# Column sums over 64 folded rows in one product, and a split reload of stored pages, in a two-layer decoder trunk

## The chip, the cores and the metric

One core of one Trainium2 chip runs the whole program. The metric is the device time of one execution in microseconds (us), the median of several executions; less is better. The kernel before has a median of 1169.38 us over 3 runs (1169.09 to 1169.43).

## What is computed

The input x is 1024 tokens by 1024 features in float32. Layer A is gated linear attention (4 heads, key width 128, value width 256, in chunks), layer B is dilated windowed attention over a shared K/V. Both end in an output product, a residual and a layer norm. What the change touches are sums over features:

```python
# layer A, per head: RMS norm of the head's 256 output features, then gain and gate, then the output product
o = o * lax.rsqrt(jnp.mean(o * o, axis=-1, keepdims=True) + RMS_EPS)
return (o.astype(x.dtype) * jax.nn.silu(g)) @ w_out

# end of both layers
x = layer_norm(DEEPNORM_ALPHA * x + y, ln_g[layer], ln_b[layer])

def layer_norm(x, g, b):
    mu = jnp.mean(x32, axis=-1, keepdims=True)
    xc = x32 - mu
    var = jnp.mean(xc * xc, axis=-1, keepdims=True)
    return xc * lax.rsqrt(var + LN_EPS) * g + b
```

## The kernel before

**Numbers.** Every large product is made from float32r halves: a value is split into a high part (`split_hi`, a copy on ACT that rounds, line 590) and a low part (`split_lo`, a subtraction on DVE or POOL, line 593), and a product is three TensorE instructions, high by high, high by low and low by high (`mm3`, line 620, and the like). Features lie on the partitions, tokens on the free axis, so a sum over features is a sum over partitions. It is made by a product with a 128x128 tile of ones, `onesr`: the tile of partial sums is split, and two products of 128x512, one for the high and one for the low part, add up in one PSUM bank (tag "ms", two buffers). The result stands in all 128 partitions.

**Where sums over partitions are made.** There are 14 of them. `chunks` (line 952) has one for each of the 4 heads and 2 chunks g of 512 tokens: the squares of the head's two output tiles are added, split and summed (lines 978 to 989); `rsqrt_rows` and a multiplication follow, and `finish` (line 995) applies gain and gate. For heads 0 to 2 the result goes to DRAM (`ogA`), for head 3 it is split at once into the pages ogh6/ogl6 and ogh7/ogl7 (the names ogh, ogl in the trace). `out_ln` (line 1035) has two for a half of 512 tokens, one for the mean (name lnA) and one for the variance, through its own `column_sums` (line 1038). It runs for both halves of layer A's end and for the first half of layer B's; the second half of layer B goes by rows (`out_ln_rows`), without such sums.

**The order of the work.** The code records operations; `Sched.order` (line 249) then places them one by one on PE, ACT, DVE, POOL and SP by its own table of costs: of all operations that are ready, the one that can start first goes next, and of several that can start at the same time the one with the lowest number in recording order. `later(n)` shifts that number. An operation recorded on `S.vp` goes to DVE or to POOL, whichever starts it earlier. So any change in one place moves instructions everywhere behind it. Projections of the next head (wA, xs) fill TensorE while a head's own chain runs on the other engines.

**The reload.** The six pages that heads 0 to 2 left in DRAM are loaded, split (ogf to ogh and ogl, kt 0 to 5) and used by layer A's output product. `reload_og` (line 1480) is called in the sequence of head 3 (letter `e`, line 1014), ahead of that head's chunks, and records both halves of 512 tokens at once with `later(-EVAC)`:

```python
for f in ('qg', 'qVg', 'qg', 'vge')[h]:
    {"g": lambda: proj_g(h), "q": lambda: proj_qk(h + 1), "V": proj_v12, "v": lambda: proj_v(3), "e": after}[f]()
for g in range(2):
    chunks(h, g)
    finish(h, g)
```

Behind it, `out_ln` of layer A runs `proj_cols` for each of 8 output tiles over kt 0 to 7 (24 products), first half first; with two "acc" banks TensorE can go through kt 0 to 5 of two tiles before it needs kt 6, which comes from head 3's first chunk. After the second half's 192 products layer B begins with `proj_v0(range(4))`, which needs the normed first half (x1h, x1l, eight pages).

Of the kernel before, what the change touches and what calls it, by code (L numbers as in the profile page):

```python
# [7 lines left out]
F32 = mybir.dt.float32  # L8
FR = mybir.dt.float32r
# [3 lines left out]
AF = mybir.ActivationFunctionType  # L13
# [5 lines left out]
GH = 4  # L19
# [556 lines left out]
def trunk(tc, xT, wP, wA, wA12, wAv3, w2, b2, ng, wO, wK, wV0, wV12, wB, wOB, lng, lnb,  # L576
# [13 lines left out]
    def split_hi(dst, src):  # L590
        S.scalar.activation(dst, src, AF.Copy)

    def split_lo(dst, src, hi):
        S.vp.tensor_sub(dst, src, hi.bitcast(F32))
# [84 lines left out]
    def load_consts():  # L679
# [3 lines left out]
        S.sync.dma_start(lngc, lng)  # L683
        S.sync.dma_start(lnbc, lnb)

    def rsqrt_rows(dst, src_ps, scale, tmp):

        S.scalar.activation(tmp, src_ps, AF.Ln, scale=scale, bias=epsc)
        S.scalar.activation(dst, tmp, AF.Exp, scale=-0.5)
# [13 lines left out]
    def layer_a(t2, t1, after):  # L703
# [116 lines left out]
        def proj_qk(h):  # L820
            new_qk(h)
            project(wA[h, 0], xs, lambda half, acc: evac_q(h, half, acc))
            project(wA[h, 1], xs, lambda half, acc: evac_k(h, half, acc))
# [22 lines left out]
        def proj_v(h):  # L846
            new_v(h)
            project_tok(wAv3, xs, [(j, lambda x, j=j: blk(x, j)) for j in range(NCH)],
                        lambda j, acc: evac_v(h, j, acc))

        def proj_g(h, cc=(0, 1)):
            if 0 in cc:
                new_sg(h)
            for c in cc:
                project(wA[h, 2 + c], xs, lambda half, acc, c=c: evac_g(h, c, half, acc))
            silu(h)
# [95 lines left out]
        def chunks(h, g):  # L952
# [27 lines left out]
                S.scalar.activation(sq[e], po[e], AF.Square)  # L980
                S.vector.tensor_copy(oT[:, e, :], po[e])
            S.vp.tensor_add(sq[0], sq[0], sq[1])
            sh, sl = (t2.tile([128, 512], FR, name="sq", bufs=3) for _ in range(2))
            split_hi(sh, sq[0])
            split_lo(sl, sq[0], sh)
            ss = ps.tile([128, 512], F32, name="ms", bufs=2)
            with S.group():
                S.tensor.matmul(ss, onesr, sh, start=True, stop=False)
                S.tensor.matmul(ss, onesr, sl, start=False, stop=True)
            R = t2.tile([128, 512], F32, name="sq", bufs=3)  # L990
            rsqrt_rows(R, ss, 1.0 / 256.0, sq[0])
            for e in range(2):
# [17 lines left out]
        for h in range(GH):  # L1010
            gate(h)
            levels(h)
            state_prep(h)
            for f in ('qg', 'qVg', 'qg', 'vge')[h]:
                {"g": lambda: proj_g(h), "q": lambda: proj_qk(h + 1), "V": proj_v12, "v": lambda: proj_v(3), "e": after}[f]()
            for g in range(2):
                chunks(h, g)
                finish(h, g)


    def small(name, tag, bufs, dt=F32, shape=(128, 512)):
# [13 lines left out]
    def out_ln(layer, r, w_of, res, emit):  # L1035
        n = r.stop - r.start

        def column_sums(x):
            hi, lo = (small("sum", "d", 4, FR)[:, :n] for _ in range(2))
            split_hi(hi, x)  # L1040
            split_lo(lo, x, hi)
            acc = ps.tile([128, 512], F32, name="ms", bufs=2)[:, :n]
            with S.group():
                S.tensor.matmul(acc, onesr, hi, start=True, stop=False)
                S.tensor.matmul(acc, onesr, lo, start=False, stop=True)
            return acc

        rt = []
# [1 line left out]
        for et in range(NK):  # L1050
# [9 lines left out]
                S.vp.tensor_add(lnA, rt[0], rt[1])  # L1060
            elif et > 1:
                S.vp.tensor_add(lnA, lnA, t)
        sm = column_sums(lnA)
        mean = small("mean", "d", 4)[:, :n]
        S.scalar.activation(mean, sm, AF.Copy, scale=1.0 / D)
        a2 = None
        for et in range(NK):
# [4 lines left out]
                a2 = s2  # L1072
            else:
                S.vp.tensor_add(a2, a2, s2)
        sv = column_sums(a2)
        R = small("R", "d", 4)[:, :n]
        t0 = small("t0", "t2", 2)[:, :n]
        rsqrt_rows(R, sv, 1.0 / D, t0)
# [398 lines left out]
        return U  # L1477


    def reload_og():  # L1480
        with S.later(-EVAC):
            for half in range(2):
                for kt in range(6):
                    load_og(ogA[kt], kt, p0, lambda: small("ogf", "a", 13), (half,))

    layer_a(t2, t1, reload_og)
    x1s = []
# [133 lines left out]
```

## Time and profile before

| | |
|---|---|
| median of 3 runs | 1169.38 us |
| the profiled execution | 1169.77 us |
| its span, first to last instruction | 1167.9 us |
| mean granted TensorE clock | 0.998 |
| PE busy | 1156.2 us, 99% |
| DVE, ACT, POOL busy | 768.3, 483.6, 162.6 us |
| chain that ended last | PE 97%, DVE 2%, DMA 1% |

The profiled execution takes 1.87 us more than its span, which lies around the program's own instructions. Matmuls are pipelined: one of 512 columns is shown with some 390 ns, and the next starts 0.227 us behind it. So what an instruction costs TensorE is read from start to start, never from the duration shown. All operations are recorded by one helper, so they share line 441, and groups are told apart by the names of their tiles.

### The profile page before, as it was taken

How to read it: one execution, taken by the hardware profiler on the slowest of the kernel's cores; microseconds unless marked ns; L12 is line 12 of the kernel's file. 1: busy time of each engine (PE TensorE's matmuls, PEld its weight loads, DVE VectorE, ACT ScalarE, POOL GpSimd, SP SyncE). 2: the span in 40 equal slices, each digit the busy share in tenths (PEclk: the TensorE clock that was granted, in tenths of full speed). 3: DMA queues.
4: the chain of work that ended last, by engine and by line, in shares of the span. 5: the costliest groups of instructions: out<-in, count | busy, mean ns of one | idle time of the engine just before them, and what ended most of it. 6: DMA issues, size and time to landing. Idle time of an engine off the chain costs nothing.

```text
span 1167.9 us, 19404 instructions
## 1 busy us (share of the span) xinstructions
PE 1156.2 (99%) x7684; PEld 981.4 (84%) x7684; DVE 768.3 (66%) x1494; ACT 483.6 (41%) x1021; POOL 162.6 (14%) x100
## 2 busy tenths in 40 slices
PE   9999999999999999999999999999999999999997
PEld 8878888889988888888888888888888888888885
DVE  6294953585867597765365657584757676647578
ACT  5364531555464345411214443435333533545242
POOL 1001000202112121221020202020212111103000
PEclk9999999999999999999999999999999999999999
DMA  7211122111143463643611111111141011134544
GB/s 251 71 38 37 56 90 76 52 56 54 57 168 112 142 208 134 198 138 106 207 47 38 46 38 55 38 50 44 38 163 38 20 38 26 32 93 145 180 145 180
DMA packets 93226, 108.17 MB, mean 93 GB/s; under 512 B 44016, under 2 KB 62064, under 8 KB 93136
## 3 DMA queue, kind: packets, MB, share of 16 engines
q1 hardware_dynamic: 93136, 106.94, 29.3%
q8 instruction: 60, 0.98, 0.4%
q14 instruction: 30, 0.25, 0.1%
HBM read 85.74 MB, written 21.17 MB: 92 GB/s over the span
## 4 chain that ended last, share of the span: by engine, by line
PE 97%; DVE 2%; DMA 1%; ACT 0%; issue 0%; SPq 0%; DVEq 0%; ACTq 0%
PE acc L441 64%; PE po L441 10%; PE lv L441 9%; PE vac L441 7%; PE ms L441 5%; PE pro L441 2%; DVE oT L441 1%; DMA xf<-in_xT 1%; DVE X L441 0%; DVE rt L441 0%; ACT sq L441 0%; SPq L441 0%; DVE b L441 0%; DVE diag L441 0%; ACT xh L441 0%
## 5 line engine op out<-in xcount | busy, mean ns | idle before, releaser
L441 PE MATMUL acc<-x1h,wh 128*128 128x512 f32 x608 | 250.5, 412 | 0.0
L441 PE MATMUL acc<-x1h,wl 128*128 128x512 f32 x608 | 237.5, 391 | 0.0
L441 PE MATMUL acc<-x1l,wh 128*128 128x512 f32 x608 | 237.0, 390 | 0.0
L441 ACT ACTIVATE wh<-wf 128x1024 fp32r<-128x1024 f32 (+2 forms) x105 | 108.5, 1034 | 294.8 <-PE acc L441 165.3
L441 POOL TENSOR_TENSOR wl<-wf,wh 128x1024 fp32r<-128x1024 f32 x39 | 93.4, 2395 | 624.0 <-ACT wh L441 488.8
L441 PEld LDWEIGHTS acc<-x1h,wl 128*128 128x128 f32 x608 | 114.1, 188 | 24.5
L441 PEld LDWEIGHTS acc<-x1l,wh 128*128 128x128 f32 x608 | 114.5, 188 | 21.3
L441 PEld LDWEIGHTS acc<-x1h,wh 128*128 128x128 f32 x608 | 114.4, 188 | 21.2
L441 DVE TENSOR_TENSOR wl<-wf,wh 128x1024 fp32r<-128x1024 f32 (+2 forms) x66 | 82.5, 1250 | 66.8 <-ACT wh L441 56.5
L441 ACT ACTIVATE P<-P,sts 128x128 f32<-128x128 f32 (+2 forms) x192 | 81.3, 425 | 63.3 <-DVE sts L441 62.9
L441 PE MATMUL acc<-xh,wh 128*128 128x512 f32 x256 | 102.5, 400 | 0.0
L441 PE MATMUL acc<-xh,wl 128*128 128x512 f32 x256 | 99.9, 390 | 0.0
L441 PE MATMUL acc<-xl,wh 128*128 128x512 f32 x256 | 99.8, 390 | 0.0
L441 DVE TENSOR_TENSOR t<-acc,cosT 128x512 f32<-128x512 f32 x60 | 41.4, 691 | 77.6 <-PE acc L441 77.4
L441 DVE TENSOR_TENSOR t<-acc,sinT 64x512 f32<-64x512 f32 x120 | 82.6, 688 | 1.6
L441 DVE CUSTOM_DVE_ANT_0 P<-lv,bmask 128x256 f32<-128x256 f32 (+1 forms) x128 | 46.8, 380 | 39.1 <-PE lv L441 38.5
L441 DVE TENSOR_TENSOR Q<-t,t 128x512 f32<-128x512 f32 x47 | 69.1, 1471 | 1.5
L441 PE MATMUL lv<-K,Q 128*64 128x64 f32 (+2 forms) x512 | 69.0, 286 | 0.0
L441 PEld LDWEIGHTS lv<-K,Q 128*128 128x128 f32 (+1 forms) x512 | 53.8, 163 | 9.7 <-issue 1.6
L441 PE MATMUL acc<-ogh,wh 128*128 128x512 f32 x152 | 60.2, 396 | 0.0
L441 PE MATMUL acc<-ogl,wh 128*128 128x512 f32 x152 | 59.4, 391 | 0.3 <-DVE ogl L441 0.2
L441 PE MATMUL acc<-ogh,wl 128*128 128x512 f32 x152 | 59.2, 390 | 0.0
(244 smaller groups left out, 2168.7 us busy)
## 6 DMA issues: line engine op xcount, KB each, us to landing
wf<-in_wB SPq DMA_DIRECT2D x32, 512.0 KB
wf<-in_wA SPq DMA_DIRECT2D x24, 512.0 KB
wf<-in_wO SPq DMA_DIRECT2D x16, 512.0 KB
wf<-in_wOB SPq DMA_DIRECT2D x16, 512.0 KB
wf<-in_wV SPq DMA_DIRECT2D x12, 512.0 KB
res<-in_xT SPq DMA_DIRECT2D x16, 256.0 KB
x1d<-rt SPq DMA_DIRECT2D x16, 256.0 KB
out<-rt SPq DMA_DIRECT2D x16, 256.0 KB
```

Of the source, the lines that this page charges most:

```text
L441: getattr(handle[o.eng], meth)(*[conv(a) for a in args], **{k: conv(v) for k, v in kw.items()})
```

## The change

`column_sums` becomes one function for both places, with a second form, `fold`. Folded, ACT copies partitions 64 to 127 of the partial sums down to 0 to 63 of a new tile, `S.vp` adds them in place, ACT makes the high part in partitions 0 to 63 of a tile `parts`, and `S.vp` writes the low part into its partitions 64 to 127. One product with the ones sums both. Ten of the 14 sums take this form: heads 0 to 2 in both chunks (6) and `out_ln` wherever the half starts at token 0 (4). Head 3 and the second half of layer A's end keep two products.

`reload_og` takes the half as an argument. The first half is recorded where both were; the second is recorded behind head 3's first chunk and its `finish`, without the shift.

```diff
+    def column_sums(acc, x, tile, fold):
+        if not fold:
+            hi, lo = tile(FR), tile(FR)
+            split_hi(hi, x)
+            split_lo(lo, x, hi)
+            with S.group():
+                S.tensor.matmul(acc, onesr, hi, start=True, stop=False)
+                S.tensor.matmul(acc, onesr, lo, start=False, stop=True)
+            return
+        t, parts = tile(F32), tile(FR)
+        S.scalar.activation(t[0:64], x[64:128], AF.Copy)
+        S.vp.tensor_add(x[0:64], x[0:64], t[0:64])
+        split_hi(parts[0:64], x[0:64])
+        S.vp.tensor_sub(parts[64:128], x[0:64], parts[0:64].bitcast(F32))
+        S.tensor.matmul(acc, onesr, parts, start=True, stop=True)
...
@@ chunks @@
-            sh, sl = (t2.tile([128, 512], FR, name="sq", bufs=3) for _ in range(2))
-            split_hi(sh, sq[0])
-            split_lo(sl, sq[0], sh)
             ss = ps.tile([128, 512], F32, name="ms", bufs=2)
-            with S.group():
-                S.tensor.matmul(ss, onesr, sh, start=True, stop=False)
-                S.tensor.matmul(ss, onesr, sl, start=False, stop=True)
+            column_sums(ss, sq[0], lambda dt: t2.tile([128, 512], dt, name="sq", bufs=3), h < GH - 1)
...
@@ layer_a, the loop over heads @@
-                {"g": lambda: proj_g(h), "q": lambda: proj_qk(h + 1), "V": proj_v12, "v": lambda: proj_v(3), "e": after}[f]()
+                {"g": lambda: proj_g(h), "q": lambda: proj_qk(h + 1), "V": proj_v12, "v": lambda: proj_v(3), "e": lambda: after(0)}[f]()
             for g in range(2):
                 chunks(h, g)
                 finish(h, g)
+                if h == GH - 1 and g == 0:
+                    after(1)
...
@@ out_ln @@
+            column_sums(acc, x, lambda dt: small("sum", "d", 4, dt)[:, :n], r.start == 0)
...
-    def reload_og():
-        with S.later(-EVAC):
-            for half in range(2):
-                for kt in range(6):
-                    load_og(ogA[kt], kt, p0, lambda: small("ogf", "a", 13), (half,))
+    def reload_og(half):
+        with S.later(0 if half else -EVAC):
+            for kt in range(6):
+                load_og(ogA[kt], kt, p0, lambda: small("ogf", "a", 13), (half,))
```

What the order makes of it is shown at three places.

**DVE, between head 2's second chunk and head 3's first level.** X on 128x8x64 is the operand of the first level's products (first from b, then times q and k); sq is the sum of squares, oT the chunk's output. Before:

```order
L441 TENSOR_TENSOR sq_2958<-sq_2909,sq_2950 128x512
L441 TENSOR_TENSOR X_2968<-b_2866 128x8x64 x2
L441 TENSOR_TENSOR X_2981<-b_2866 128x16x32
L441 COPY v_2885<-acc_2941 128x256
L441 TENSOR_TENSOR oT_2926<-oT_2926,sq_2987 128x512 x2
L441 SCALAR_TENSOR_TENSOR oT_2926<-oT_2926,ngc_120,sg_2553 128x512 x2
L441 TENSOR_TENSOR X_2968<-X_2968,q_2247 128x8x64
L441 TENSOR_TENSOR X_2968<-X_2968,k_2351 128x8x64
```

The change:

```order
L441 TENSOR_TENSOR X_2979<-b_2870 128x8x64
L441 COPY v_2888<-acc_2913 128x256
L441 TENSOR_TENSOR X_2979<-b_2870 128x8x64
L441 TENSOR_TENSOR X_3009<-b_2870 128x16x32
L441 TENSOR_TENSOR sq_3004<-sq_2941,sq_3004 64x512
L441 TENSOR_TENSOR X_3009<-b_2870 128x16x32
L441 TENSOR_TENSOR X_2979<-X_2979,q_2214 128x8x64
L441 TENSOR_TENSOR X_2979<-X_2979,k_2357 128x8x64
```

The four operations on oT that stood ahead of X's products with q and k stand behind them; the low part of the squares has 64 rows.

**DVE, head 3's first chunk.** ogl0 to ogl5 are low parts of reloaded pages, S the state, sq the squares, oT the chunk's output. Before:

```order
L441 TENSOR_TENSOR ogl2_3537<-ogf_3488,ogh2_3535 128x512
L441 TENSOR_TENSOR ogl3_3544<-ogf_3493,ogh3_3542 128x512
L441 TENSOR_TENSOR ogl4_3554<-ogf_3495,ogh4_3549 128x512
L441 TENSOR_TENSOR ogl5_3561<-ogf_3500,ogh5_3556 128x512
L441 COPY oT_3638<-po_3563 128x512
L441 COPY oT_3638<-po_3567 128x512
L441 TENSOR_TENSOR sq_3657<-sq_3630,sq_3651 128x512
L441 SCALAR_TENSOR_TENSOR S_3672<-S_3613,dec_3106,ms_3665 128x256
L441 SCALAR_TENSOR_TENSOR S_3677<-S_3672,dec_3106,ms_3674 128x256
L441 TENSOR_TENSOR oT_3638<-oT_3638,sq_3681 128x512 x2
```

The change (the copies of oT and one S stand right ahead of these rows):

```order
L441 TENSOR_TENSOR ogl5_3627<-ogf_3508,ogh5_3619 128x512
L441 TENSOR_TENSOR sq_3609<-sq_3609,sq_3624 128x512
L441 TENSOR_TENSOR ogl0_3529<-ogf_3513,ogh0_3520 128x512
L441 TENSOR_TENSOR ogl1_3542<-ogf_3515,ogh1_3533 128x512
L441 TENSOR_TENSOR sq_3650<-sq_3609,sq_3643 128x512
L441 TENSOR_TENSOR ogl2_3559<-ogf_3522,ogh2_3549 128x512
L441 TENSOR_TENSOR ogl3_3591<-ogf_3524,ogh3_3567 128x512
L441 TENSOR_TENSOR ogl4_3615<-ogf_3531,ogh4_3602 128x512
L441 SCALAR_TENSOR_TENSOR S_3672<-S_3617,dec_3351,ms_3662 128x256
L441 TENSOR_TENSOR oT_3598<-oT_3598,sq_3679 128x512
```

The second half's pages no longer stand ahead of the chunk's copies but between the sum of squares and the multiplication by its inverse root.

**PE, the start of layer B.** wh and wl are weights, x1h and x1l the normed pages 0 to 7 of the first half; acc and vac are two projections' banks. Before:

```order
L441 MATMUL acc_4389<-wh_4336,x1h7_4381 128x256
L441 MATMUL acc_4389<-wl_4356,x1h7_4381 128x256
L441 MATMUL acc_4389<-wh_4336,x1l7_4395 128x256
L441 MATMUL acc_4425<-wh_4284,x1h0_4210 128x256
L441 MATMUL acc_4425<-wl_4303,x1h0_4210 128x256
```

The change:

```order
L441 MATMUL vac_4466<-wh_4388,x1h0_4238 128x512
L441 MATMUL vac_4466<-wl_4403,x1h0_4238 128x512
L441 MATMUL vac_4466<-wh_4388,x1l0_4256 128x512
L441 MATMUL acc_4381<-wh_4332,x1h7_4452 128x256
L441 MATMUL acc_4381<-wl_4345,x1h7_4452 128x256
L441 MATMUL acc_4381<-wh_4332,x1l7_4462 128x256
L441 MATMUL ms_4473<-sum_4456,onesr_99 128x512
L441 MATMUL ms_4473<-sum_4464,onesr_99 128x512
```

Before, page 7 is read after 21 products of the first token group; now after 42 products (two groups, pages 0 to 6) and 9 of another projection (vac).

## Rows read from the trace of the kernel before

**Rows 1.** The page: busy time by engine, and the granted clock in 40 slices.

```profile
PE 1156.2 (99%) x7684; PEld 981.4 (84%) x7684; DVE 768.3 (66%) x1494; ACT 483.6 (41%) x1021; POOL 162.6 (14%) x100
...
PEclk9999999999999999999999999999999999999999
```

**Rows 2.** Who PE waited for, whole span: total us, times, longest.

```profile
PE pro L441 <- DVE Dg L441: 1.2, 1, 1.2
PE pro L441 <- ACT xh L441: 1.2, 1, 1.2
PE lv L441 <- DVE mn L441: 0.6, 1, 0.6
PE lv L441 <- DVE X L441: 0.5, 1, 0.5
PE acc L441 <- DVE ogl L441: 0.2, 1, 0.2
```

**Rows 3.** Tile ms on PE: products with the ones; count, ns, first and last start.

```profile
L441 PE MATMUL ms<-sq,onesr x16: 392/395/399, 116.6 to 361.3; 128*128 128x512 f32 x16
L441 PE MATMUL ms<-sum,onesr x12: 397/399/497, 397.6 to 1137.3; 128*128 128x512 f32 x12
```

**Rows 4.** Order of time, PE, one variance sum: start, us, instruction, count.

```profile
416.25 0.39 PE L441 MATMUL acc<-ogh,wl 128*128 128x512 f32 x1
416.48 0.64 PE L441 MATMUL ms<-sum,onesr 128*128 128x512 f32 x2
416.95 0.39 PE L441 MATMUL acc<-ogh,wh 128*128 128x512 f32 x1
```

**Rows 5.** Groups by shape, whole span: full and half height; mean ns behind the comma.

```profile
L441 DVE TENSOR_TENSOR t<-acc,sinT 64x512 f32<-64x512 f32 x120 | 82.6, 688 | 1.6
L441 DVE TENSOR_TENSOR t<-acc,cosT 128x512 f32<-128x512 f32 x60 | 41.4, 691 | 77.6 <-PE acc L441 77.4
L441 ACT ACTIVATE sq<-sq 128x512 fp32r<-128x512 f32 x8 | 5.0, 625 | 3.8 <-POOL sq L441 3.0 <-DVE sq L441 0.9
```

**Rows 6.** Order of time, all engines, head 3's first level.

```profile
298.44 1.78 DVE L441 SCALAR_TENSOR_TENSOR oT<-oT,ngc,sg 128x512 f32<-128x512 f32 x1
...
300.74 0.68 DVE L441 TENSOR_TENSOR X<-X,k 128x512 f32<-128x512 f32 x1
300.81 0.28 PE L441 MATMUL acc<-wh,xl 128*128 128x256 f32 x1
...
301.57 0.65 PE L441 MATMUL lv<-X 128*64 128x64 f32 x15 [0.48 <-DVE X L441]
```

**Rows 7.** Order of time, POOL, the same stretch.

```profile
297.99 1.68 POOL L441 TENSOR_TENSOR X<-X,k 128x512 f32<-128x512 f32 x1 [3.42 <-ACT X L441]
```

**Rows 8.** Order of time, head 3's first chunk to page kt 7.

```profile
343.17 2.17 ACT L441 ACTIVATE ogh<-ogf 128x512 fp32r<-128x512 f32 x4
...
343.64 0.60 PE L441 MATMUL po<-qe,S 128*128 128x128 f32 x4
...
345.25 1.06 ACT L441 ACTIVATE sq<-po 128x512 f32<-128x512 f32 x2
...
357.00 0.19 PEld L441 LDWEIGHTS acc<-ogl,wh 128*128 128x128 f32 x1 [0.49 <-POOL ogl L441]
...
358.45 0.19 PEld L441 LDWEIGHTS acc<-ogl,wh 128*128 128x128 f32 x1 [0.54 <-DVE ogl L441]
```

**Rows 9.** Order of time, the start of layer B.

```profile
438.05 0.28 PE L441 MATMUL acc<-wh,x1h 128*128 128x256 f32 x1
...
438.63 1.74 POOL L441 TENSOR_TENSOR x1l<-rt,x1h 128x512 fp32r<-128x512 f32 x1 [2.69 <-ACT x1h L441]
...
440.57 0.28 PE L441 MATMUL acc<-wh,x1h 128*128 128x256 f32 x1
```

**Rows 10.** Order of time, DVE, layer B's end.

```profile
1135.85 0.69 DVE L441 TENSOR_TENSOR sum<-sq,sum 128x512 fp32r<-128x512 f32 x1 [0.70 <-ACT sum L441]
1137.23 0.69 DVE L441 SCALAR_TENSOR_TENSOR rt<-res,acc 128x512 f32<-128x512 f32 x1 [0.69 <-DMA res<-x1t]
...
1157.67 1.41 DVE L441 SCALAR_TENSOR_TENSOR rt<-rt,lnR,bet 128x512 f32<-128x512 f32 x2
1160.23 0.69 DVE L441 SCALAR_TENSOR_TENSOR rt<-res,acc 128x512 f32<-128x512 f32 x1 [1.15 <-PE acc L441]
```

**Rows 11.** Order of time, DVE, behind the first half's variance in layer A.

```profile
422.80 1.70 DVE L441 TENSOR_TENSOR wl<-wf,wh 128x1024 fp32r<-128x1024 f32 x1
424.42 1.77 DVE L441 TENSOR_TENSOR x1l<-rt,x1h 128x512 fp32r<-128x512 f32 x1
...
429.68 1.22 DVE L441 TENSOR_TENSOR wl<-wf,wh 128x1024 fp32r<-128x1024 f32 x1
430.81 0.69 DVE L441 TENSOR_TENSOR x1l<-rt,x1h 128x512 fp32r<-128x512 f32 x1
```

**Rows 12.** Order of time, POOL, the same stretch.

```profile
423.38 2.27 POOL L441 TENSOR_TENSOR lnA<-lnA,rt 128x512 f32<-128x512 f32 x1
```

More of the change, by code (lines that the diff above doesn't have):

```diff
@@ L1036, in out_ln, with sums @@
         n = r.stop - r.start
[L1038 to L1041, printed above, removed]
+        def sums(x):
             acc = ps.tile([128, 512], F32, name="ms", bufs=2)[:, :n]
-            with S.group():
-                S.tensor.matmul(acc, onesr, hi, start=True, stop=False)
-                S.tensor.matmul(acc, onesr, lo, start=False, stop=True)
+            column_sums(acc, x, lambda dt: small("sum", "d", 4, dt)[:, :n], r.start == 0)
             return acc
@@ L1062, in out_ln @@
                 S.vp.tensor_add(lnA, lnA, t)
-        sm = column_sums(lnA)
+        sm = sums(lnA)
         mean = small("mean", "d", 4)[:, :n]
@@ L1074, in out_ln @@
                 S.vp.tensor_add(a2, a2, s2)
-        sv = column_sums(a2)
+        sv = sums(a2)
         R = small("R", "d", 4)[:, :n]
```

## The prediction, made before the change was run

> **What bounds the kernel now.** I began with the page: PE is busy for 99% of the span at a granted clock that never leaves the full 2.4 GHz level, DVE for 66%, ACT for 41% [rows 1]. Busy time of a pipelined engine proves little, so the list of PE's waits came next: five waits, 3.7 us of 1167.9, and 2.4 of them at the start [rows 2]. TensorE issues all but without a break from 10 us to 1160 us. A change can therefore win in three ways only: fewer products, fewer of the small waits, or a shorter end behind the last product. And whatever it adds on DVE, ACT or POOL is free until a product has to wait for it.
>
> **Fewer products.** The trace has 28 products with the ones, two for each of 14 sums [rows 3]. Their price is not the 395 ns shown but the start of the next instruction: a pair begins at 416.48 and the next product at 416.95 [rows 4], so one costs 0.235 us, close to the 0.227 from one ordinary product to the next. Ten go: 10 x 0.235 = 2.35 us off PE. The sum over 128 rows of mixed parts costs what the sum over 128 high parts did, since 512 columns pass either way.
>
> **What they are bought with.** A folded sum has one more ACT copy and one more addition on DVE or POOL. Half the rows are no cheaper: 64x512 takes 688 ns on DVE, 128x512 takes 691; for ACT I take the 625 ns of the full tile [rows 5]. A sum comes later by 0.63 + 0.69 and two hand-overs of some 0.05: about 1.4 us. For heads 0 to 2 the order answers with more work in front: 18 projection products where 9 stood ahead of the first chunk's sum, 2.0 us more against the 1.4. I cost these six at nothing; without that cover it would be up to 6 x 1.4 = 8.4 us. DVE's and POOL's 10 x 0.69 = 6.9 us spread over a DVE with a third of its time free.
>
> **Head 3's first level.** The last projection product starts at 300.81 and has some 0.12 us of issue; the level starts at 301.57, so PE loses 0.64 us, to X times k, which ends at 301.42 [rows 6]. DVE was late since two multiplications of oT stood ahead, one of them 1.78 us long. It ran beside a POOL instruction of 297.99 to 299.67 [rows 7]: 299.67 plus a half-microsecond of own work gives its end. The Trainium skill (SBUF — State Buffer, Who interferes with whom) has a rule for it: a DVE instruction with two SBUF inputs and a POOL instruction that reads SBUF exclude each other for a whole instruction; the trace agrees here, with the 1.78. In the change's order X's two products stand ahead of the oT group, which is worth 3 us to them; on the other side the chunk's sum is 1.4 us longer, and PE comes to the level about 1.1 us earlier against the head's gate. I walk that row by row with the durations above and find X ready 0.3 us ahead of its need. So the wait should mostly go. Bounds: -0.64, and +0.6 if POOL's 64-row halves hold DVE once more; I take -0.4.
>
> **The reload.** Head 3's first chunk ends on PE at about 344.2, but its squares start on ACT only at 345.25, behind four copies of reloaded pages [rows 8]; DVE's low parts of the same pages stand ahead of the chunk's copies likewise. At the end of this chain PE waits twice, for ogl of kt 6 and of kt 7: 0.23 and 0.50 us beyond the usual interval (loads of weights are held for 0.49 and 0.54). With the second half's pages behind the sum of squares, the chain starts 1 us earlier; five pages then stand between the sum and the multiplication by the inverse root, but ACT needs some 2 us there for the root and its table. PE also asks for kt 6 some 1.5 us later, by the products that stand ahead of it in its order. Bounds: 0 and -0.73; I take -0.6.
>
> **Layer A's end.** Both sums of the first half come 1.4 us later, 2.8 together, and PE is at layer B 0.47 us sooner. Page 7 was ready at 440.37, and its low part was asked for 0.24 behind 440.57 [rows 9]: 0.4 us to spare. But the order now puts 42 products of 0.12 and 9 of 0.227, 7.1 us, ahead of page 7 where there were 21 x 0.12 = 2.5. Spare: 0.4 + 4.6 - 0.5 - 2.8 = 1.7 us. I cost it at nothing; bound +2.9 (below).
>
> **The end of the kernel.** DVE's own queue nearly fills layer B's end: behind the low part of the second sum at 1135.85 it has 0.69 us of waiting for a residual and 1.15 us in front of the last tile [rows 10]. The second folded sum is a bare chain: ACT, DVE, ACT, DVE, so DVE is 1.4 us later; of the first sum, weight splits fill the gap and only the added 0.69 counts. 2.1 us against 0.69 + 1.15 + about 0.2 of small gaps, less the 0.47 by which PE ends sooner: 1.6. Some 0.3 to 0.5 us come out, I take +0.3; bounds 0 (if more is filled) and +1.5 (both chains in full).
>
> **The sum.** -2.35 - 0.4 - 0.6 + 0.3 = -3.05 us. The profiled execution took 1169.77, so 1166.7; it lay 0.39 above the median of the three runs, so 1166.3. A measurement of this kernel can tell about 0.2% from no change, 2.34 us: faster means under 1167.04, slower over 1171.72. The forecast clears that by less than a microsecond.
>
> **The rivals.**
>
> *Head 3 keeps its waits.* The order is fuller around head 3, and where POOL's halves hold DVE the level is late again; the reload's second half may delay the chain as much as it did from the front. For it: spares of 0.3 us in a walk with 0.1 us errors. Against it: the oT group is out of the way. Both middle terms are then 0: -2.35 + 0.3, or 1167.3. By the skill's rule named above, any POOL half that starts just ahead of X costs its whole length: 1.28 to 1.5 us instead of a share; it is one more reason for this case.
>
> *The longer sums come out: slower than before.* Place: the first half's pages at the start of layer B. The change's order leaves three additions to lnA with POOL in this stretch. In the trace such an addition of 2.27 us [rows 12] stretched two DVE instructions beside it, from 1.22 to 1.70 and from 0.69 to 1.77: 1.56 us lost [rows 11]. Three of them, 4.7, with the 2.8 of the sums is 7.5 against a cover of 0.4 + 4.6 - 0.5 = 4.5: PE waits up to 2.9 us, and up to 1.5 more come out at the end. It decides once the chain is more than 4.5 us later. With the middle terms at 0 that is -2.35 + 2.9 + 1.5 = +2.05, 1171.4; in part, anything from 1168 on. Against it: three holds of full length have to meet.
>
> *The products saved are given back.* PE is filled by a planner that puts each product just ahead of its need, so that the chains on DVE set the pace where PE is early: ten new delays of 1.4 us need only lose 0.2 each. Time 1168.5 to 1169.4. Against it: before, with the same planner, only two such waits appeared in the whole middle [rows 2].
>
> **How the numbers follow.** Forecast 0.55, head 3's waits 0.25, longer sums 0.08, given back 0.12. Faster by over 0.2%: nine tenths of the forecast and a third of the second case, 0.59. Slower: the upper part of the third, 0.03. The rest, 0.38, is within. The forecast's own span is 1165.3 (both waits gone, nothing at the end, and 0.3 of luck) to 1167.5; the range goes on to 1168.8, through the second case and half of the last. Left out are the longer sums, the rest of the last case and a little below.
>
> **What would show it.** 18 products with the ones instead of 28, and PE's busy time less by some 2 us. No wait of PE on X near 300 us or on ogl near 357 us, and no new one on x1l near 440 us; the idle time of DVE ahead of the last tile near 0 instead of 1.15 us. The working is wrong if PE's issue from 10 us to its last product is not shorter by 2 to 3.5 us; if it is, and the time is not, the end is what I mis-sized.

## The result, and the profile after

| | median of 15 runs | lowest to highest | profiled execution |
|---|---|---|---|
| before | 1169.73 us | 1169.09 to 1171.49 | 1169.77 us, span 1167.9 |
| changed | 1171.48 us | 1170.22 to 1174.99 | 1170.41 us, span 1168.6 |

The ratio is 1.0017, 95% interval 1.0011 to 1.0024: about 2 us slower, where 3 us less had been forecast, and above the top of the range, 1168.8. Two single executions of kernels further below, one of layer B alone (4425 us) and one of the change without layer A's fold (4123 us), are left out of every ratio. Two things stand out before any view is read. The changed kernel's runs spread over 4.8 us where those of before spread over 2.4, and its profiled execution was its second fastest. A trace of one execution will therefore show less than the median has lost.

The page of the changed kernel, to be read against [rows 1] (in the rows, PE is TensorE, PEld its weight loads, DVE VectorE, ACT ScalarE and POOL GpSimd):

```profile
PE 1153.6 (99%) x7674; PEld 979.3 (84%) x7674; DVE 782.0 (67%) x1510; ACT 488.3 (42%) x1027; POOL 161.1 (14%) x98
```

PE has 10 products less and 2.6 us less of busy time, at the same clock (mean granted clock 0.997; 0.998 before). The products with the ones, against [rows 3]:

```profile
L441 PE MATMUL ms<-sq,onesr x10: 390/398/498, 117.9 to 359.7; 128*128 128x512 f32 x10
L441 PE MATMUL ms<-sum,onesr x8: 392/397/399, 397.3 to 1139.6; 128*128 128x512 f32 x8
```

18 instead of 28, as the change says. Now the list of PE's waits, which was the second view before [rows 2]:

```profile
PE acc L441 <- DVE rt L441: 1.6, 1, 1.6
PE pro L441 <- DVE Dg L441: 1.2, 1, 1.2
PE pro L441 <- ACT xh L441: 1.0, 1, 1.0
PE lv L441 <- issue: 0.9, 1, 0.9
PE lv L441 <- DVE mn L441: 0.6, 1, 0.6
PE ms L441 <- DVE sq L441: 0.4, 1, 0.4
```

The waits on ogl and on X are gone from the list. Three are new: 1.6 us for a VectorE instruction `rt`, 0.9 us on "issue", and 0.4 us on `sq`. The first is at the place where layer A gives way to layer B. PE's weight loads there, in order of time (start, duration, and in brackets the idle time before and its releaser):

```profile
437.51 0.19 PEld L441 LDWEIGHTS acc<-wh,x1l 128*128 128x128 f32 x1
439.56 0.19 PEld L441 LDWEIGHTS acc<-wh,x1h 128*128 128x128 f32 x1 [1.85 <-DVE rt L441]
```

and VectorE and GpSimd in the stretch before it:

```profile
421.23 2.52 DVE L441 TENSOR_TENSOR x1l<-rt,x1h 128x512 fp32r<-128x512 f32 x1
423.67 1.77 DVE L441 TENSOR_TENSOR rt<-rt,R 128x512 f32<-128x512 f32 x1
...
428.28 2.38 DVE L441 TENSOR_TENSOR x1l<-rt,x1h 128x512 fp32r<-128x512 f32 x2
...
433.85 2.07 DVE L441 TENSOR_TENSOR wl<-wf,wh 128x1024 fp32r<-128x1024 f32 x1 [0.46 <-ACT wh L441]
435.84 1.28 DVE L441 TENSOR_TENSOR x1l<-rt,x1h 128x512 fp32r<-128x512 f32 x2
...
438.82 0.68 DVE L441 SCALAR_TENSOR_TENSOR rt<-res,acc 128x512 f32<-128x512 f32 x1
```

```profile
420.80 2.40 POOL L441 TENSOR_TENSOR wl<-wf,wh 128x1024 fp32r<-128x1024 f32 x1 [9.74 <-ACT wh L441]
423.16 1.74 POOL L441 TENSOR_TENSOR lnA<-lnA,rt 128x512 f32<-128x512 f32 x1
427.37 2.14 POOL L441 TENSOR_TENSOR lnA<-lnA,rt 128x512 f32<-128x512 f32 x1 [2.47 <-DVE rt L441]
...
433.53 1.30 POOL L441 TENSOR_TENSOR lnA<-lnA,rt 128x512 f32<-128x512 f32 x1 [1.62 <-DVE rt L441]
```

The product at 439.56 opens the second of the two acc buffers. The changed order puts pages 0 to 4 for that buffer directly behind pages 0 to 4 for the first. But the buffer still holds the last tile of the output projection, and the VectorE instruction that takes it out is the row at 438.82, which ends at 439.50. It stands behind a queue that GpSimd has lengthened: 2.52 us for an x1l that takes 0.69 alone [rows 11], 1.77 for a product with R that takes 0.68, 2.38 for two x1l where two others, from 435.84, take 1.28, and 2.07 for a wl that takes 1.22. That is 1.83 + 1.09 + 1.10 + 0.85 = 4.9 us, each time beside a GpSimd instruction that had begun first, and VectorE's own ended 0.5 to 1.1 us behind it.

The wait itself is made of two things. The same row of the kernel before:

```profile
439.13 0.68 DVE L441 SCALAR_TENSOR_TENSOR rt<-res,acc 128x512 f32<-128x512 f32 x1
```

Counted from the first product of layer B (438.05 us before, 435.96 now), VectorE had emptied that buffer after 1.76 us and now has after 3.54. And PE asked for it behind 24 products of 0.12 us, 2.88 us, and now asks behind 15, 1.79 us. So VectorE comes 1.8 us later and PE 1.1 us sooner, against a spare of 1.1: a wait of 1.8 us. With the old 24 products ahead, some 0.7 of it would have been left.

The second new wait is in the level products of head 3; the row at 319.11 is the last of 128:

```profile
316.82 1.35 PE L441 MATMUL lv<-X 128*32 128x32 f32 x127
319.11 0.22 PE L441 MATMUL lv<-X 128*32 128x32 f32 x1 [0.94 <-issue]
```

And the end of the kernel, on VectorE, against [rows 10]:

```profile
1160.48 0.68 DVE L441 SCALAR_TENSOR_TENSOR rt<-res,acc 128x512 f32<-128x512 f32 x1
```

VectorE no longer idles ahead of the last tile, and starts it 0.25 us later than before.

**Where the time went.** Since the start of an execution varies (the first gate product of head 0, up to which all these kernels run the same instructions, came between 1.40 us earlier and 1.48 us later than in the trace of before), I count from that product. The table gives how much later (+) or earlier (-) the same PE product, or VectorE's last tile, came than in the trace of before, less the difference at the gate. The last column is the start of the first reload transfer, ogf.

| trace | head 3's gate, 279 us | output projection, 388 | layer B, 578 | last product | last tile on VectorE | first ogf at |
|---|---|---|---|---|---|---|
| before | 0 | 0 | 0 | 0 | 0 | 327.3 |
| changed | -1.06 | -0.88 | +0.73 | +0.26 | +1.01 | 332.1 |
| changed, second profile | -1.07 | -1.37 | -0.06 | -0.51 | +0.25 | 331.3 |
| reload alone | +0.12 | -1.14 | -1.15 | -0.90 | -0.90 | 326.0 |
| heads alone | -1.05 | +2.85 | +2.85 | +2.93 | +2.93 | 332.0 |
| layer A alone | +0.04 | -0.09 | +1.62 | +1.85 | +1.84 | 327.0 |
| layer B alone | -0.05 | -0.17 | -0.17 | +0.69 | +1.42 | 326.6 |
| heads and reload | -1.11 | +1.35 | +1.35 | +1.34 | +1.35 | 332.1 |
| changed, without layer A | -1.09 | +1.48 | +1.48 | +1.77 | +2.83 | 331.9 |
| heads 0 and 1, and reload | -1.13 | -2.38 | -2.38 | -2.38 | -2.38 | 326.6 |
| products for nothing | -0.91 | -1.79 | -1.40 | -1.78 | -1.78 | 327.3 |
| heads and reload, shifted program | -1.18 | -1.15 | -1.07 | -1.12 | -1.13 | 337.9 |

The lower rows are of the experiments below. Up to head 3's gate the four products of heads 0 and 1 come off in full (4 x 0.235 = 0.94). From there to 388 us the change should gain another 0.47 for head 2 and 0.73 for the reload, and instead loses 0.2; the second profile, with luck that the last run below explains, gains 0.3. At the border of the layers it loses 1.6 more.

### The profile page after: what moved, and what is told of

It is laid out like the page before. It is cut to its first block, busy times and chain, and to the rows that moved or that the text cites. A ratio compares the mean times of both kernels' runs of the same rounds, so it can differ in the third digit from the quotient of the medians.

```text
span 1168.6 us, 19387 instructions
## 1 busy us (share of the span) xinstructions
PE 1153.6 (99%) x7674; PEld 979.3 (84%) x7674; DVE 782.0 (67%) x1510; ACT 488.3 (42%) x1027; POOL 161.1 (14%) x98
## 4 chain that ended last, share of the span: by engine, by line
PE 95%; DVE 3%; DMA 0%; issue 0%; ACT 0%; SPq 0%; DVEq 0%; ACTq 0%
PE acc L441 62%; PE po L441 10%; PE lv L441 9%; PE vac L441 7%; PE ms L441 4%; PE pro L441 2%; DVE rt L441 1%; DVE x1l L441 1%; DMA xf<-in_xT 0%; DVE X L441 0%; DVE wl L441 0%; DVE oT L441 0%; ACT wh L441 0%; SPq L441 0%; DVE lnst L441 0%
## 5 line engine op out<-in xcount | busy, mean ns | idle before, releaser
L441 POOL TENSOR_TENSOR wl<-wf,wh 128x1024 fp32r<-128x1024 f32 x40 | 96.1, 2403 | 594.2 <-ACT wh L441 461.0
```

The source lines that it names most:

```text
L441: getattr(handle[o.eng], meth)(*[conv(a) for a in args], **{k: conv(v) for k, v in kw.items()})
```

## The experiments

Theory 1: the loss sits at two places, layer A's border and the stretch between head 2's sums and the reload. Theory 2: PE runs so close to its feeders that every saving is given back as waits. Theory 3 was first the end of the kernel, later the length of the folded sums' chains. Medians are of 5 to 11 runs, those of before of 23 to 33; every ratio is against before on the same chip.

### One part at a time

The reload split alone:

```diff
-            column_sums(ss, sq[0], lambda dt: ..., h < GH - 1)
+            column_sums(ss, sq[0], lambda dt: ..., False)
-            column_sums(acc, x, lambda dt: ..., r.start == 0)
+            column_sums(acc, x, lambda dt: ..., False)
```

> Only the reload is split; all 14 sums keep two products. Theory 1 (what the change gains up to 430 us is lost where layer A gives way to layer B, through the two folded sums there): the two waits on ogl near 357 us are gone and nothing else moves, -0.5 to -0.7 us against before. Theory 2 (every part gives back what it saves, because the planner brings each product up to its need): the waits turn up elsewhere, -0.2 to +0.2 us. Theory 3 (the end of the kernel takes it all): -0.5 to -0.7 us, as theory 1.

1168.11 us, ratio 0.9989 (0.9980 to 0.9998). By the ratio that is 1.3 us less (0.2 to 2.3), and the waits on ogl are gone from its trace. This part of the change is good by itself; the interval holds the 0.5 to 0.7 us of theory 1.

The heads' six sums alone (reload as before, `False` in `out_ln`):

> Only the six sums of heads 0 to 2 are folded, reload as before: 22 products with the ones. Theory 1: six products less, 6 x 0.235 = 1.41, head 3's waits about as before (+0.2): -1.2 us; if the 1.1 us gap in the level products at 318 us belongs to this order and not to chance, -0.1 us. Theory 2: -0.2 to +0.2 us. Theory 3: -1.2 us.

1174.40 us, ratio 1.0042 (1.0029 to 1.0054): nearly 5 us slower, which no theory had. Its waits, beyond those of before and the waits on issue and `sq` that the changed kernel has (0.6 and 0.4 us here):

```profile
PE ms L441 <- DVE S L441: 1.2, 1, 1.2
PE acc L441 <- ACT ogh L441: 1.0, 1, 1.0
PE acc L441 <- POOL ogl L441: 0.8, 1, 0.8
```

All three belong to the reload: its first transfer starts at 332.0 us, not 327.3. The cause is upstream. In this order, as in that of the whole change, head 3's last level comes 4.8 us later (4.9 in the changed kernel), and by the kernel's pools the reload's pages lie where head 3's level tiles lay: in each trace the first transfer begins within 0.1 us of the end of PE's last transposition of head 3's `ke`. In the changed kernel's trace the last X of head 3 is one of the steps that came late (VectorE, and GpSimd beside it):

```profile
325.66 2.89 DVE L441 TENSOR_TENSOR X<-X,k 128x512 f32<-128x512 f32 x1
```

```profile
325.28 2.72 POOL L441 TENSOR_TENSOR wl<-wf,wh 128x1024 fp32r<-128x1024 f32 x1 [14.46 <-ACT wh L441]
```

Layer A's two sums alone (heads `False`, `layer == 0 and r.start == 0`), and layer B's two alone:

> Only the two sums of layer A's first half are folded: 26 products with the ones. Theory 1: two products less (-0.47) and a wait of PE for the second acc bank near 438 us of 1.8 to 2.1 us: +1.3 to +1.6 us. Theory 2: -0.2 to +0.2 us. Theory 3: -0.5 us.

> Only the two sums of layer B's first half are folded: 26 products with the ones. Theory 1: PE's last product 0.47 us earlier, DVE's last tile 0.25 us later, as in the changed kernel's trace: +0.2 to +0.3 us. Theory 2: 0. Theory 3: +1.5 us or more.

Layer A: 1171.77 us, ratio 1.0023 (1.0013 to 1.0033), theory 1 and rather more than its 1.3 to 1.6 us (2.7 by the ratio, 1.5 to 3.9): the same wait for the second acc buffer, 1.8 us in the list, at the same place. Layer B: 1170.09 us, ratio 1.0005 (0.9996 to 1.0014), not to be told from no change, and the +0.2 to +0.3 expected lies within. Its trace, though, doesn't show what was expected: PE's last product comes 0.69 us later, not 0.47 sooner, behind a wait in layer B's end (0.6 us in the list, on the low part `wol` of the output weights) that neither trace of the changed kernel has. VectorE's last tile is later than the last product by another 0.73.

### Do the parts add?

The heads and the reload; then the change without layer A:

> The six sums of heads 0 to 2 folded and the reload split; both layer norms keep two products per sum. Theory 1 (the heads' folded sums make head 3's last level, and with it the first reload transfer, about 5 us later; that hurts only while all twelve pages stand ahead of head 3's first squares, so the split cures it): 6 x 0.235 = 1.41 less, the two waits on ogl gone, head 3's waits +0.2, the gap of about 1.1 us in the level products at 318 us stays, some 0.3 us more at 339: -0.6 to -1.3 us against before. Theory 2 (the costs of the parts simply add: +4.8 and -1.5): +3.3 us.

> The change without the fold of layer A's two sums. Theory 1: as the run before with layer B's +0.2 to +0.5 us: -0.8 to 0 us against before. Theory 2: +3.8 us.

1170.79 us, ratio 1.0010 (1.0001 to 1.0019), and 1170.83 us, ratio 1.0009 (1.0000 to 1.0018). The truth lies between: the split of the reload cures most of what the heads lose (not +3.3), but not all (not -0.6). What is left shows in both traces as a wait of about 2 us at 339 us that the trace of the changed kernel does not have. VectorE of the heads-and-reload kernel there:

```profile
336.64 0.69 DVE L441 TENSOR_TENSOR ogl<-ogf,ogh 128x512 fp32r<-128x512 f32 x1 [0.16 <-ACT ogh L441]
339.56 0.69 DVE L441 TENSOR_TENSOR ogl<-ogf,ogh 128x512 fp32r<-128x512 f32 x1 [2.23 <-ACT ogh L441]
340.17 0.68 DVE L441 COPY sg<-acc 128x512 f32<-128x512 f32 x1
340.77 0.41 DVE L441 COPY S<-ms 128x256 f32<-128x256 f32 x1
```

ScalarE's third copy in that kernel:

```profile
338.90 0.63 ACT L441 ACTIVATE ogh<-ogf 128x512 fp32r<-128x512 f32 x1 [2.29 <-PE po L441]
```

and VectorE of the changed kernel, with the same instructions in the same order:

```profile
336.67 1.38 DVE L441 TENSOR_TENSOR ogl<-ogf,ogh 128x512 fp32r<-128x512 f32 x2 [0.23 <-ACT ogh L441]
337.96 0.68 DVE L441 COPY sg<-acc 128x512 f32<-128x512 f32 x1
338.56 0.41 DVE L441 COPY S<-ms 128x256 f32<-128x256 f32 x1
```

Three pages' low parts stand ahead of head 3's first state copy S, on which PE's next products wait. ScalarE's copy of the third page, which VectorE needs, started 0.7 us behind that of the second in one execution and 2.9 us in the other. It was the transfer, although the row names PE: the last of the third page's 16 parts landed at 336.60 us in the changed kernel and at 338.82 in this one (338.63 in the trace without layer A, where the other 15 were there by 336.70), and the copy started 0.08 to 0.09 us behind it each time. With the reload 5 us later, that landing decides.

Heads 0 and 1 and the reload (`h < GH - 2`, `False` in `out_ln`):

> Sums folded in heads 0 and 1 alone, and the reload split. Theory 1 (a folded sum costs nothing where projection products cover it, and what heads 0 to 2 lost came from head 2's sums alone, which stand right ahead of head 3): four products less, 0.94, on top of the reload's 1.3 to 1.5: -2.2 to -2.5 us against before, no gap at 318 us, reload transfers start at about 326 us as before. Theory 2 (each folded sum of a head loses the same): the loss of the heads alone, 4.8, by two thirds, less 1.5: +1.7 us.

1167.77 us, ratio 0.9986 (0.9977 to 0.9994), theory 1: -1.6 us by the ratio (-0.7 to -2.7), and in its trace 2.38 earlier at the last product, counted from the gate. Its waits, all of them known from [rows 2]:

```profile
PE pro L441 <- ACT xh L441: 1.9, 1, 1.9
PE pro L441 <- DVE Dg L441: 1.2, 1, 1.2
PE lv L441 <- DVE mn L441: 0.6, 1, 0.6
PE lv L441 <- DVE X L441: 0.5, 1, 0.5
```

The reload starts at 326.6 us again. So it is head 2's two sums, right ahead of head 3, that push the reload; the other four cost nothing that shows in the trace.

### Layer A's border: holds or chains?

```diff
-                S.vp.tensor_add(lnA, lnA, t)
+                (S.vp if layer else S.vector).tensor_add(lnA, lnA, t)
...
-        split_lo(lo, wf, hi)
+        (lo_on or S.vp).tensor_sub(lo, wf, hi.bitcast(F32))
```

(the second for the output weights, and in the same way for the low parts of x1; on top of the kernel with layer A's sums alone)

> As the kernel with layer A's two sums alone folded (+2.2 us), but in layer A's output norm the running sums lnA, the low parts of x1 and the low parts of the output weights run on VectorE alone, so that GpSimd holds no VectorE instruction there. Theory 1 (VectorE is late at the border because it is held by GpSimd, 4 us in the stretch, and not because two sums are 1.4 us longer): PE's wait of 1.9 us for the second acc bank shrinks to under 0.6, total +0.6 us or less against before. Theory 3 (the longer chains of the two sums are what makes it late): the wait stays, +1.8 us or more.

1171.34 us, ratio 1.0018 (1.0009 to 1.0027). The wait at the border is gone altogether, with the folded sums and their chains as long as before. But the kernel gains nothing: two new waits come at 479 and 490 us.

```profile
PE ms L441 <- DMA x1f<-x1d: 1.2, 1, 1.2
PE acc L441 <- DVE t L441: 1.1, 1, 1.1
```

For the wait at the border this speaks against the longer chains alone. It does not show that the holds alone made it, for they are fewer here but not gone: two low parts of layer B's own weights, at 433.26 and 438.14 us on GpSimd, make two x1l of VectorE last 2.19 and 2.43 us, one of them ahead of the emptying of the buffer. VectorE was still done with it 1.54 us behind layer B's first product (437.02), so PE would not have waited behind five pages (1.80 us) either, and the six that stand ahead of it in this order are not what cured it. But VectorE's own queue has another order too, and holds and order were not separated. For the time, theory 1 missed; 1.2 us of it went in layer B's end (below). The opposite edit put three of the sums lnA of layer A's second half on GpSimd, in the kernel before:

> The kernel before, no fold and the old reload, but three of the running sums lnA of layer A's second half (tiles 4 to 6) are put on GpSimd, as the changed order has them. Theory 1 (holds make VectorE late at the border): more time of VectorE held between 415 and 440 us than the 2.1 us of before, and PE waits there by 0.5 to 2 us: +0.5 to +2 us against before. Theory 3 (the length of the folded sums' chains does it): no new wait of PE, 0 to -0.3 us.

1171.17 us, ratio 1.0016 (1.0008 to 1.0025). The size is that of theory 1, the mechanism another. VectorE was held no more than before; GpSimd's own queue became late. GpSimd, and PE's load that waited for it:

```profile
440.08 1.30 POOL L441 TENSOR_TENSOR lnA<-lnA,rt 128x512 f32<-128x512 f32 x1 [3.55 <-DVE lnA L441]
441.34 2.54 POOL L441 TENSOR_TENSOR x1l<-rt,x1h 128x512 fp32r<-128x512 f32 x1
```

```profile
443.93 0.19 PEld L441 LDWEIGHTS acc<-wh,x1l 128*128 128x128 f32 x1 [1.66 <-POOL x1l L441]
```

This run shows that the border has no room: without any fold, one more addition ahead of an x1l in GpSimd's queue, which had stood 3.55 us for VectorE's lnA, costs PE 1.5 us. (The trace is of the slowest of its 11 runs, 1173.89 us; 0.9 us more went in layer B's end.)

### What are ten products worth when nothing is paid?

```diff
-        t, parts = tile(F32), tile(FR)
...
-        S.tensor.matmul(acc, onesr, parts, start=True, stop=True)
+        hi = tile(FR)
+        split_hi(hi, x)
+        S.tensor.matmul(acc, onesr, hi, start=True, stop=True)
```

> As the change, but the ten folded sums are replaced by one product over the high parts alone: no fold, no low part, so the low parts of these ten sums are left out of the result. It shows what ten products less are worth when nothing is paid for them. Theory 1 (the products' 0.235 us each are real, and what the change lost was paid with the longer chains): 10 x 0.235 = 2.35 less and the reload's 1.3 to 1.5, so -3.2 to -3.9 us against before; up to 1 us less of a gain if a burst of level products meets a block of instructions that is late. Theory 2 (PE is so close to its feeders that time saved on products comes out as waits even then): -1.5 us or less of a gain.

1168.16 us, ratio 0.9985 (0.9976 to 0.9994): some 1.75 us of gain (0.7 to 2.8), nearer to theory 2's 1.5 or less than to theory 1's 3.2 or more, and within the intervals no more than the reload's split alone (1.3). Against [rows 2] one wait has grown and one is new:

```profile
PE lv L441 <- DVE X L441: 1.3, 1, 1.3
...
PE ms L441 <- DVE sum L441: 0.6, 1, 0.6
```

Counted from the gate, this trace is 0.91 earlier at head 3's gate, as four products should be, and the wait for X has grown from 0.5 to 1.3 behind it. Here PE did arrive early, and waited for VectorE. This run says most: in the order that this kernel gets, most of the 2.35 us were not there even when nothing was paid for them.

### The waits that come and go

Heads and reload, with 24 small products more in the start-up, so that later instructions stand further on in PE's program (the trace shows 48 products and 48 weight loads more, two of each for one product); then with the reload's first half planned later; then both:

```diff
+            for _ in range(24):
+                S.tensor.matmul(accs[7][:, 0:32], ..., start=True, stop=True)
...
-            S.sync.dma_start(f, src[:, hs(half)])
+            with S.landing(1.0 if pool is p0 and half == 0 else 0.0):
+                S.sync.dma_start(f, src[:, hs(half)])
```

> As the kernel with heads folded and reload split (+1.2 us), with 24 small products more of PE in the start-up, where PE waits for its first input, so that all later instructions stand 48 places further on in PE's program. Theory 1 (the gap of 0.9 us inside the level's 128 products at 318 us is the wait for the next block of instructions, whose transfer is asked for only as the burst begins, at 316.8 us): the gap is gone or at another burst; -0.9 us against the unshifted kernel if gone. Theory 4 (the gap belongs to a semaphore or an input of that product): it stays at 318 us.

> As the kernel with heads folded and reload split (+1.2 us), but the planner is told that each reload transfer of the first half takes 1 us longer, so that on VectorE one page's low part stands ahead of head 3's first state copy where three stood. Theory 1 (PE's wait of 2.1 us at 339 us is the third page's landing, behind which the state copies stand; it is there in some executions and not in others): the wait is gone, -1.5 to -2.1 us against that kernel, -0.3 to -0.9 against before, and the runs lie closer together. Theory 2: the wait only moves, no gain.

> Both cures on the kernel with heads folded and reload split: the program shifted by 24 small products and the reload's transfers planned 1 us longer. Theory 1: six products less (1.41), reload 1.3, head 3's waits +0.2: -1.5 to -2.4 us against before. Theory 2: no better than the better of the two cures alone.

The shifted program took 1176.47 us, ratio 1.0056 (1.0045 to 1.0068), because the shift itself was dear: head 0's gate came 6.3 us later. Counted from the gate its last product is 2.46 us earlier than in the unshifted kernel. The gap at 318 us is gone: the transfer of instructions ahead of that burst now began 7.3 us before it. The wait for the state copy is 0.9 instead of 2.1. So the total missed and the mechanism held. Later pages: 1171.40 us, ratio 1.0012 (1.0003 to 1.0021), theory 2: the wait at 339 went, and 2 us of waits on the chunk's squares (0.55), ogh (0.48) and ogl (0.98) came at 350 to 359; the gap at 318 was 1.8 us this time. Both: 1178.85 us, ratio 1.0075 (1.0062 to 1.0089), with the gate 10.2 us later; neither wait is in its trace, and those of the later pages are. Counted from the gate its last product is 0.11 us earlier than before, where the shift alone has 1.12. It bought nothing.

At last the best kernel with head 3's X on VectorE alone, and the changed kernel once more:

```diff
-                    S.vp.tensor_mul(Xv[:, :, 0, :], Xv[:, :, 0, :], view(k)[:, :, 0, :])
+                    (S.vp if h < GH - 1 else S.vector).tensor_mul(Xv[:, :, 0, :], ...)
```

(and the same for the subtraction that makes this half of X)

> As the kernel with heads 0 and 1 folded and the reload split (-1.85 us), and in head 3's levels both halves of X stay on VectorE, so that GpSimd holds nothing there. Theory 1 (the wait of 0.6 us on X is GpSimd's hold): the wait shrinks by half or more, -2.1 to -2.6 us against before. Theory 2 (VectorE is full there, whoever does it): the wait grows by the two or three instructions that VectorE does in addition, 0.6 us or more, -1.2 us or worse.

> The changed kernel once more, for its spread and a second profile. Theory 1: the waits at 297, 300, 318 and 438 us are there again (0.6, 0.3, about 1 and about 1.8 us); at 339 us a wait of up to 2.1 us on the state copy if the third page lands late. Time as before, +1.5 to +2.3 us. If the wait at 339 us never shows, the rest of its time is not explained by it.

The first: 1167.74 us, ratio 0.9984 (0.9976 to 0.9993). The wait on X is gone, theory 1, but the time is that of the kernel without the edit: a wait of 0.4 us for a state came in its place, and 1.2 us were lost in layer B's end. The second: 1172.40 us, ratio 1.0034 (1.0023 to 1.0046), 4.0 us slower (2.7 to 5.4) where 1.5 to 2.3 had been expected. The profiled execution took 1169.92, the fastest of its seven (up to 1175.80). In that one, neither chance wait is there. The level products ran through:

```profile
317.10 1.37 PE L441 MATMUL lv<-X 128*32 128x32 f32 x128
```

and the wait for S at 339 us was 0.2. The wait at the border is there again, 1.4 us in the list. The program is the same; the traffic was not. In the first profile of the changed kernel a transfer of the instruction queue falls into 316 to 318 us (it starts at 316.8, as the burst does):

```profile
q8 instruction: 1, 0.02, 3.0%
```

In the second there is none between 316 and 318: it started at 312.1. The wait at 339 us is in neither of the two traces of the changed kernel, so what its slower executions lose was not seen.

A third place of this kind is in layer B's end, between 1115 and 1137 us, where PE waits for low parts of the output weights (`wol`) whose transfers landed late, and in some traces for the sums beside them. It cost 1.3 us in all in the trace of layer B alone, 1.2 in that with layer A's additions on VectorE and in that with X on VectorE, 0.9 in that with three lnA on GpSimd, 0.7 in the change without layer A and 0.5 with later pages. It is in neither trace of the changed kernel and not in that of before, and it comes with layer B's fold and without it.

## Why the prediction was wrong

**Fewer products, -2.35.** The price of a product was right: four came off by 1.06 us up to head 3's gate, and layer A's two by 0.47. What was wrong is the first paragraph's conclusion, that a PE that issues all but without a break keeps what is taken off it. By the prediction's own sign it is the working that failed: nearly every other sign came true (18 products, 2.6 us less of busy time, no wait on ogl or x1l, no idle time ahead of the last tile), but from head 0's gate to the last product PE takes 0.3 us more, not 2 to 3.5 less. Dropped for nothing, the ten products gained hardly more than the reload alone. Rival 3, with a chance of 0.12, said so, though its time of at most 1169.4 was too low. Its reason was right for head 3 and the border; heads 0 and 1 keep theirs, as the run with these two shows.

**The heads' six at nothing.** This is the first step of the sum that failed. It held for heads 0 and 1. For head 2 the cover of 2.0 us of products was looked at for its sums alone, and the instructions behind them on VectorE were not: head 3's levels came out up to 4.9 us later, and with them the first reload transfer. The second sum came late by itself too (0.56 us at 297).

**Head 3's first level, -0.4.** Missed: 0.64 became 0.26, but the sum's 0.56 stands ahead of it, so +0.18. The bound of +0.6 for half-height instructions on GpSimd held it.

**The reload, -0.6.** The two waits went, 0.73 us, and alone the split gained more than that by its median and its trace (0.90 at the last product). But the step took the start of the transfers as given, and the heads' fold moves it by 5 us: a change whose two parts I costed apart was not two parts.

**Layer A's end, nothing.** The second step that failed, and the largest in the trace: 1.8 and 1.5 us. The spare of 1.7 was worked out for page 7 alone, and counted 7.1 us of products ahead of it as cover. Five triples of them write the second acc buffer, and they cannot start before VectorE has emptied it, which the order asks for 1.1 us sooner and VectorE does 1.8 us later. Cover that itself waits for the late engine is no cover. The rival "the longer sums come out" had the place, the engine and the price (up to 2.9 us). That its full price gives 1171.4, next to the median, is luck: it has nothing of what head 2 lost. I gave it 0.08, because three holds of full length "have to meet". They met, though at the second buffer and not at page 7, and in all three traces with this fold and lnA on GpSimd PE waits there: 1.6, 1.4 and 1.8 us. By the Trainium skill (SBUF — State Buffer, Who interferes with whom) a VectorE instruction with two SBUF inputs and a GpSimd instruction that reads SBUF exclude each other for a whole instruction; the rows at 421 to 436 us agree, with 2.52 us for 0.69, and I had used the rule at head 3 alone.

**The end, +0.3.** The mechanism held, the size did not. The term was what comes out behind a last product that is 0.47 sooner. Against the last product VectorE's last tile moved by 1.01 - 0.26 = +0.75 in the first trace, +0.76 in the second, and by 0.73 and 1.06 in the traces of layer B alone and without layer A: more than twice the term, within its bounds of 0 and +1.5.

**What the sum lacked altogether** is the waits of chance, 0 to 1.1 us at 318 (1.8 with later pages), 0 to 2.1 us at 339 and 0 to 1.3 us in layer B's end, seen in some traces of these orders and not in that of before. They would fit the wider spread of the runs and the median's standing 1.07 us above the first profiled execution and 2.5 above the second; but only the first of the three was seen in the changed kernel itself, and how often each comes was not counted. So of the 1.75 us by which the medians differ the first trace accounts for 0.64, the difference of the two profiled executions, and the rest stays open. Open too is why the transfer of a block of instructions begins early in one execution and late in another, and why a page lands early or late.

Two sums of the prediction have slips that change little: 7.5 - 4.5 is 3.0 and not 2.9 (the rival of the longer sums), and nine tenths of 0.55 with a third of 0.25 are 0.58 and not 0.59.

## What to carry to other kernels

Where a planner sets the order, PE's busy share says little about who sets the pace: before a product is counted as gain, look for the next place where another engine's queue ends just in time, and ask whether the time saved survives it. Cover counts only if it can start without the engine that is late, buffers included; follow what is queued behind an added instruction to the first transfer that it releases. Of this change, the split of the reload with the folds of heads 0 and 1 is worth keeping (1167.77 against 1169.62 us); the rest is not. That the two folds add to the split is seen in the traces (2.38 us earlier at the last product against 0.90), not in the times, whose intervals overlap.

## What the runs showed of the hardware

The 128 level products in quarter tiles and their weight loads run through in 1.4 us. Where the transfer of the next 16 KB of PE's instructions began only with the burst, 0.2 us ahead of it to 0.6 behind its start, PE stood for 0.8 to 1.8 us (five traces, each with head 2 folded; in the first of the changed kernel the transfer began at 316.8), and the product behind the gap came 2.2 to 2.4 us after the transfer's start in all five. It did not stand where the transfer began 2.5 us or more ahead (nine traces; before: transfer at 314.0, burst at 316.5). The Trainium skill (Runtime: NRT & Kernel Launch, Instruction fetch mechanics) calls the crossing of such a block mostly hidden; here it was not.

A float32 product of 32 columns over a full 128x128 tile is not small: each of the two instructions that the trace shows for it took 0.112 us from start to start, as those of 128 columns do, so the 24 of the shift took 5 us and more. In that stretch of the shifted program the granted clock fell to the level of 1.2 GHz, and these instructions then took 0.212 us:

```profile
0.00:5.00 5.00, 3.76 (x11) 1.00 0.59 167
5.00:10.00 5.00, 5.00 (x39) 0.81 0.88 285
10.00:15.00 5.00, 5.00 (x24) 0.50 0.97 336
15.00:20.00 5.00, 5.00 (x42) 1.00 0.80 282
```

(stretch, its length, PE's busy time and count, the granted clock, 0.50 being the lower level, the share of time that the transfers were busy, and their GB/s; the first stretch's clock rests on readings from 4.73 us on). PE had run some 30 of the 48 instructions of 32 columns before it fell. That these products made it fall is not shown: in the run with three lnA on GpSimd, which has none of them, the clock fell too, from 11.4 to 14.8 us.
